# Attention by halves of the queries, with half of the output product fed into it

## The chip, the cores and the metric

The kernel runs on one NeuronCore of a Trainium2 chip. The metric is the device time of one execution in microseconds (us), lower is better. All data are float32.

## The reference, cut to what matters

One hybrid layer on 1024 tokens of width 1024. A norm and one input projection feed two branches: a bidirectional state-space (SSM) branch in chunks of 128, and windowed attention with 16 query heads over 4 key heads. Both are gated and normed, concatenated (2048 columns), multiplied by `w_out` (2048 x 1024), added to the input and normed once more.

```python
h = rms_norm(x, norm_in_g)
z, xbc, dt_raw, q, k, v, ga = split(h @ w_in)
...
def block(idx):                      # 128 queries see 384 keys
    logits = einsum('bqkgd,btkd->bkgqt', qb, kb) * scale + bias
    logits = where(valid, logits, NEG_INF)
    m = maximum(max(logits), sink)
    p = exp(logits - m)
    denom = sum(p) + exp(sink - m)
    return einsum('bkgqt,btkd->bqkgd', p, vb) / denom
...
y_attn = rms_norm(o * silu(ga), attn_norm_g)
return rms_norm(x + concat([y_ssd, y_attn]) @ w_out, final_norm_g)
```

Keys and values of a key head serve 4 query heads. The 8 query blocks of 128 tokens need the keys of their own block and of its two neighbours.

## The kernel before, in words

Engines: TensorE (PE) for matmuls and transposes, VectorE (DVE), ScalarE (ACT), GpSimd (POOL), and SyncE (SP), whose queue issues nearly all DMAs. Each engine and each queue works in order. The orders on DVE, ACT, POOL and SP are set by a planner that simulates the whole program and gives each engine, whenever it is free, the earliest traced instruction that is ready in the simulation. In the attention stage the order on PE is written out by hand: `pe` (L773) ties every matmul behind the one before.

Products are made in float32r: each operand is split into a rounded `hi` and a rest `lo`, and three matmuls (hi hi, hi lo, lo hi) make one product.

Stages:

1. Norm of x, projections by blocks of 128 output columns (`proj_steps`, L147; 24 matmuls of 128x512 per half of the tokens), SSM branch with convolutions. Projections of the gates and of q and k are pulled forward into the SSM stage by `fill`. What comes from the branches goes to DRAM (`z_d`, `ga_d`, `q_d`, `k_d`, `v_d`, `y_d`).
2. Attention: 32 steps, for each key head `kv` (outer) and each query block `qb` (inner). A `Step` loads its queries (`qt`, L824), and per key head `load_kv` (L753) loads keys twice (once for each half of the partitions), values and bias into two rotating buffers; `vz` (L889) holds one half of the values with zeros beside. `logits` (L838): 2 matmuls (L850), DVE adds bias and takes the maximum into `nm` (L853), ACT makes the exponential and its sum into `sm` (L856); four times per step. `denominators` (L859): sink exponential, sum and reciprocal (L861 to L865), once per step. `transpose` (L867), `weigh` (values, L898) and `collect` (L903) into `og`.
3. After every 4 query blocks, `gate(kv, hf)` (L912): the reciprocals are transposed on PE (L917), copied by ACT (L919), written to DRAM from POOL (L920), read back to all partitions (L924), and POOL multiplies gate, reciprocal and `og` (L928, L929), squares (L930) and sums the squares over heads into `sqa` (L933 to L936). `store` (L939) puts `og` to `o_d`; with the last key head it marks the half as stored (`stored`).
4. Output. `outputs` (L640) is a generator. Its first half, 2 x 8 row blocks x 2 halves of the columns with 12 matmuls each, multiplies the SSM part of `w_out` and adds it to `accs`, which hold x. The second half, for each row block `sb`, waits until its half of attention is stored (L694), sums `sqa` over channels (L699), multiplies 48 matmuls (L658) with `o_d` rows that `parts` (L646) splits, adds (L707), squares (L709) and norms (L119 on POOL, L730 on DVE).
5. `chore` (L419) splits 128x512 pieces of `w_out` (ACT L429, DVE L430, loads L416 through three buffers) into the space that the projection's inputs leave: 32 pieces, of which the last 8 may be made only when the SSM half of the product is done (`chores_up_to(32)`, L692).

Each step follows the string `STEP` (L398): `q` logits of the next step, `t` transposes, `w` values, `s` one chore, `g` the gate of a finished half, `d` the denominators of the next step, `c` collect, and `f4` a share of the step's feed. `feed` (L782) pulls matmuls out of the projections that are left and then out of `outputs`, and counts matmuls; `QUOTA` (L393) of them go into each step, and `FIRST` behind each of the four first logits. Whatever is not fed by then follows attention (`feed(100000)`, L985).

```python
    steps = [(kv, qb) for kv in range(NKV) for qb in range(NSB)]
    ...
        if pending and qb % 4 == 2:
            store()
        if qb % 4 == 3:
            done = kv, qb // 4
    ...
    gate(*done)
    store()
    feed(100000)
```

Of the kernel before, what the change touches and what calls it, by code (L numbers as in the profile page):

```python
# [16 lines left out]
P = 128  # L17
# [18 lines left out]
def kernel(  # L36
# [356 lines left out]
    PRE, QUOTA, FIRST, RB = 1, 17, 2, 3  # L393
# [4 lines left out]
    STEP = "q0 q1 f4 t1 s f3 t2 f4 q2 f3 t0 f4 q3 w1 g f4 w2 s f4 d w0 c"  # L398
# [241 lines left out]
    def outputs():  # L640
# [47 lines left out]
        fg = at.tile([P, D], F32, tag="khh", name="fg")  # L688
        nc.sync.dma_start(out=fg, in_=bass.AP(tensor=fin_g.tensor, offset=fin_g.offset, ap=[[0, P], [1, D]]))
        junk = at.tile([P, D], F32, tag="kll", name="junk")  # L690
# [62 lines left out]
    def load_kv(kv):  # L753
        khh = at.tile([P, S], F32R, tag="khh", name="khh")
        kll = at.tile([P, S], F32R, tag="kll", name="kll")
        for t, hl in ((khh, 0), (kll, 1)):
            for half in range(2):
                nc.sync.dma_start(out=t[half * 64:(half + 1) * 64, :].bitcast(F32), in_=k_d[hl, kv])
        vt = at.tile([P, NSB, P], F32R, tag="vt", name="vt")
        nc.sync.dma_start(out=vt.bitcast(F32), in_=v_d[kv].rearrange("b t c -> t b c"))  # L760
        bias = at.tile([P, 2, 320], F32, tag="bias", name="bias")
        for h in range(4):
            r = rep_d[kv * 4 + h, 0:1, 127:447]
            nc.sync.dma_start(out=bias[(h % 2) * 64:(h % 2 + 1) * 64, h // 2, :],
                              in_=bass.AP(tensor=r.tensor, offset=r.offset, ap=[[511, 64], [1, 320]]))
        return khh, kll, vt, bias
# [33 lines left out]
    vz = [at.tile([P, NSB, P], F32R, name=f"vz{i}", bufs=1) for i in range(2)]  # L800
# [10 lines left out]
    def half_tiles(kv, hf):  # L811
        sm = sqp.tile([P, 16], F32, tag="sm", name="sm", bufs=2)
        og = sqp.tile([P, 4, 2, P], F32, tag="og", name="og", bufs=2)
        return sm, og

    class Step:


        def __init__(self, kv, qb):
            self.kv, self.qb = kv, qb  # L820
            if kv not in kvs:
                kvs[kv] = load_kv(kv)
            self.qt = at.tile([P, 2, 4, 64], F32R, tag="qt", name="qt", bufs=2)
            nc.sync.dma_start(out=self.qt.rearrange("p s h q -> p (s h q)").bitcast(F32),  # L824
                              in_=q_d[kv, :, :, 2 * qb:2 * qb + 2].rearrange("i d s h q -> (i d) (s h q)"))
            self.lg = lgs[(kv * NSB + qb) % 2]
            self.nm = at.tile([P, 4], F32, tag="nm", name="nm", bufs=3)
            if qb % 4 == 0:
                halves[kv, qb // 4] = half_tiles(kv, qb // 4)
            self.sm = halves[kv, qb // 4][0].rearrange("p (b c s) -> p b c s", b=2, c=4)[:, :, qb % 4, :]  # L830

            self.lo, self.hi = lo, hi = qb > 0, qb < NSB - 1
            self.groups = [[(256, 384 if lo else 320)],
                           [(0, 128, 0, qb - 1)] * lo + [(128, 256, 0, qb)],
                           [(384, 512, 1, qb)] + [(512, 640, 1, qb + 1)] * hi]
            self.tr = {}

        def logits(self, k):  # L838
            kv, qb = self.kv, self.qb
            khh, kll, vt, bias = kvs[kv]  # L840
# [6 lines left out]
            k0 = (qb - 1) * P + c0  # L847
            ps = bank("s")
            for i, kt in enumerate((khh, kll)):
# [5 lines left out]
                                   accum_out=self.nm[:, k:k + 1])  # L855
            A.activation(out=l, in_=l, func=AF.Exp, scale=-1.0,  # L856
                         bias=self.nm[:, k:k + 1], accum_out=self.sm[:, hp, sub:sub + 1])

        def denominators(self):  # L859
            n2 = self.nm.rearrange("p (b s) -> p b s", b=2)  # L860
            V.tensor_tensor(out=n2, in0=n2, op=ALU.add,  # L861
                            in1=snk[:, 2 * self.kv:2 * self.kv + 2].unsqueeze(2).broadcast_to([P, 2, 2]))
            A.activation(out=self.nm, in_=self.nm, func=AF.Exp)
            V.tensor_tensor(out=self.sm, in0=self.sm, in1=n2, op=ALU.add)
            V.reciprocal(out=self.sm, in_=self.sm)  # L865
# [16 lines left out]
        def weigh(self, i):  # L882
            vt, qb = kvs[self.kv][2], self.qb
            if i == 1:
                self.po = bank("y")
                if qb == 0:
                    for half, t in enumerate(vz):
                        h = slice(half * 64, (half + 1) * 64)
                        nc.sync.dma_start(out=t[h].bitcast(F32), in_=v_d[self.kv, :, h].rearrange("b t c -> t b c"))  # L889

            if i > 0:
                prods = [(g[2], vt[:, g[3], :], j * 256) for j, g in enumerate(self.groups[i])]
            else:
                prods = [(0, vz[0][0:P if self.lo else 64, qb + 1, :], 0)] if self.hi else []
                prods += [(1, vz[1][:, qb - 1, :], 0)] if self.lo else []
# [7 lines left out]
        def collect(self):  # L903
            pov = self.po.rearrange("p (s b a q) -> p b s a q", s=2, b=2, a=2)
            c = self.qb % 4
            og = halves[self.kv, self.qb // 4][1][:, c].rearrange("p b (s q) -> p b s q", s=2)
# [5 lines left out]
    def gate(kv, hf):  # L912
        sm, og = halves[kv, hf]
# [32 lines left out]
    steps = [(kv, qb) for kv in range(NKV) for qb in range(NSB)]  # L946
# [4 lines left out]
    cur.denominators()  # L951
    done = None
    total = sum(int(t[1:]) for t in STEP.split() if t[0] == "f")
    for n, (kv, qb) in enumerate(steps):
        nxt = Step(*steps[n + 1]) if n + 1 < len(steps) else None
        fed = part = 0
        for t in STEP.split():
# [7 lines left out]
            elif t[0] == "d" and nxt:  # L965
                nxt.denominators()
# [72 lines left out]
```

## Time and profile before

| what | us |
|---|---|
| median of 3 runs | 922.18 |
| lowest and highest | 919.39, 931.5 |
| the profiled execution's own time | 922.42 |
| its span in the profile | 920.6 |

The profile is of one execution. Times in it count from the start of the span. An engine's busy time is the sum of its instructions; matmuls are pipelined, so their durations overlap, and the distance from one start to the next is what each takes. "PEld" is PE's loading of weights. "L147" is a line of the kernel, and "<-" after an idle time names what ended it. The granted clock of PE is given as a share of its full speed, over the whole span 0.978.

### The profile page before, as it was taken

Reading aid. Unit: us, or ns where it says so; the run is one execution under the profiler, and the core shown is the slowest. Engines: PE = TensorE matmul, PEld = TensorE weight load, DVE = VectorE, ACT = ScalarE, POOL = GpSimd, SP = SyncE. Lnnn points to the kernel's source line nnn. Section 1 sums busy time; section 2 is a strip of 40 time slices with the busy share of each in tenths; the row PEclk is TensorE's granted clock in tenths of the full one; section 3 lists DMA queues with packets and bytes.
Section 4 is the critical chain, followed back from the end, with each engine's and each line's share of the span. In section 5 each row is a group of like instructions: output and inputs, shape, how many; then the busy total and the mean of one; then the engine's idle time right before and its main releaser. Section 6 shows DMA issues by size and latency. Waiting matters only on the chain.

```text
span 920.6 us, 13289 instructions
## 1 busy us (share of the span) xinstructions
PE 852.7 (93%) x4622; PEld 717.1 (78%) x4622; DVE 652.0 (71%) x1108; ACT 472.8 (51%) x1102; POOL 325.4 (35%) x258
## 2 busy tenths in 40 slices
PE   6799999998699999999979978988889999999997
PEld 5798788886577888888757856867778878888886
DVE  6475674696798466458989815796888998896433
ACT  7442573453566345434745515766656767662222
POOL 2201012645777100245598630140341342345001
PEclk9999999999999999999998998999999999999999
DMA  7232554675768412678868668369838464343321
GB/s 282 63 92 57 190 179 162 210 228 173 224 224 267 114 46 91 186 227 227 258 206 253 190 202 218 98 179 290 245 95 216 122 193 124 111 142 121 106 95 57
DMA packets 137407, 155.67 MB, mean 169 GB/s; under 512 B 44235, under 2 KB 93259, under 8 KB 137212
## 3 DMA queue, kind: packets, MB, share of 16 engines
q1 hardware_dynamic: 135660, 150.30, 53.7%
q0 software_dynamic: 1536, 4.26, 1.8%
q8 instruction: 36, 0.59, 0.3%
q14 instruction: 31, 0.25, 0.1%
q10 hardware_dynamic: 144, 0.26, 0.1%
HBM read 112.49 MB, written 44.40 MB: 170 GB/s over the span
## 4 chain that ended last, share of the span: by engine, by line
PE 67%; DVE 15%; DMA 9%; issue 4%; ACT 2%; SPq 1%; POOL 1%; DVEq 0%; POOLq 0%; ACTq 0%
PE mm L147 34%; PE mm L658 16%; PE y L898 4%; PE s L850 3%; PE mm L284 3%; DMA cb<-cs_d 2%; DMA snk<-in_sink_dram 2%; DMA oraw<-in_w_out_dram 2%; DVE M L583 2%; PE t L873 2%; PE s L533 1%; DVE pl L879 1%; PE s L515 1%; DVE lg L853 1%; DVE M L584 1%
## 5 line engine op out<-in xcount | busy, mean ns | idle before, releaser
L147 PE MATMUL mm<-hlo,whi 128*128 128x512 f32 (+1 forms) x640 | 248.7, 390 | 5.8 <-DVE hlo L210 5.1
L147 PE MATMUL mm<-hhi,whi 128*128 128x512 f32 (+1 forms) x640 | 249.2, 392 | 0.0
L147 PE MATMUL mm<-hhi,wlo 128*128 128x512 f32 (+1 forms) x640 | 248.1, 389 | 0.0
L147 PEld LDWEIGHTS mm<-hlo,whi 128*128 128x128 f32 x640 | 122.7, 192 | 28.7 <-DVE hlo L210 5.8
L147 PEld LDWEIGHTS mm<-hhi,wlo 128*128 128x128 f32 x640 | 122.9, 192 | 21.9 <-issue 0.7
L147 PEld LDWEIGHTS mm<-hhi,whi 128*128 128x128 f32 x640 | 122.5, 192 | 21.6 <-issue 0.7
L658 PE MATMUL mm<-hhi,yh 128*128 128x512 f32 (+1 forms) x264 | 104.0, 394 | 0.0
L658 PE MATMUL mm<-hhi,yl 128*128 128x512 f32 (+1 forms) x264 | 104.0, 394 | 0.0
L658 PE MATMUL mm<-hlo,yh 128*128 128x512 f32 (+1 forms) x264 | 103.9, 394 | 0.0
L856 ACT ACTIVATE lg<-lg,nm 128x320 f32<-128x320 f32 (+2 forms) x128 | 68.9, 539 | 49.5 <-DVE nm L853 47.3
L243 DVE SCALAR_TENSOR_TENSOR acc<-pad,prm_sb,acc 128x1024 f32<-128x1024 f32 x48 | 62.3, 1301 | 27.1 <-ACT acc L240 25.8
L853 DVE CUSTOM_DVE_ANT_0 lg<-s,bias,nsnk 128x320 f32<-128x320 f32 (+2 forms) x128 | 64.5, 517 | 20.5 <-PE s L850 20.3
L138 POOL TENSOR_TENSOR wlo<-wraw,whi 128x1024 fp32r<-128x1024 f32 x12 | 30.7, 2560 | 106.1 <-ACT whi L135 106.1
L135 ACT ACTIVATE whi<-wraw 128x1024 fp32r<-128x1024 f32 x38 | 40.2, 1057 | 49.0 <-PE mm L147 46.7
L574 ACT ACTIVATE cb<-cb,ncs 128x128 f32<-128x128 f32 x128 | 39.3, 389 | 32.8 <-DMA cb<-cs_d 32.7
L138 DVE TENSOR_TENSOR wlo<-wraw,whi 128x1024 fp32r<-128x1024 f32 x26 | 36.9, 1418 | 26.7 <-ACT whi L135 26.5
L658 PEld LDWEIGHTS mm<-hhi,yh 128*128 128x128 f32 x264 | 49.9, 189 | 5.9
L658 PEld LDWEIGHTS mm<-hlo,yh 128*128 128x128 f32 x264 | 49.9, 189 | 5.8
L850 PE MATMUL s<-khh,qt 128*128 128x320 f32 (+1 forms) x128 | 39.5, 314 | 16.0 <-DMA qt<-q_d 10.8
L658 PEld LDWEIGHTS mm<-hhi,yl 128*128 128x128 f32 x264 | 49.9, 189 | 5.6
L879 DVE TENSOR_TENSOR pl<-t,ph 128x512 fp32r<-128x512 f32 (+1 forms) x64 | 41.1, 653 | 5.6 <-ACT ph L878 5.1
L235 POOL MEMSET pad<- 128x2 f32 x12 | 1.4, 117 | 123.1 <-DMA dx_d<-pad 65.3
(223 smaller groups left out, 1825.3 us busy)
## 6 DMA issues: line engine op xcount, KB each, us to landing
wraw<-in_w_blk_dram SPq DMA_DIRECT2D x38, 512.0 KB, 4.1
cb<-cs_d SPq DMA_DIRECT2D x32, 512.0 KB, 5.5
oraw<-in_w_out_dram SPq DMA_DIRECT2D x32, 256.0 KB, 4.5
qt<-q_d SPq DMA_DIRECT2D x32, 256.0 KB, 3.4
et<-es_d SPq DMA_DIRECT2D x56, 128.0 KB, 4.0
dx_d<-pad SPq DMA_DIRECT2D x8, 512.0 KB, 4.3
z_d<-gz SPq DMA_DIRECT2D x16, 256.0 KB, 2.6
yb<-dx_d SPq DMA_DIRECT2D x16, 256.0 KB, 3.1
```

The costliest lines, as they stand in the source:

```text
L135: A.activation(out=hi, in_=raw, func=AF.Copy)
L138: eng.tensor_tensor(out=lo, in0=raw, in1=hi.bitcast(F32), op=ALU.subtract)
L147: yield T.matmul(ps, lhsT=l[:, kb, :], rhs=r[sh][:, kb, cols], start=(n == 0), stop=(n == 3 * NKB - 1))
L243: V.scalar_tensor_tensor(out=acc, in0=pad[:, k:k + S], scalar=cw[:, blk * 6 + k:blk * 6 + k + 1], in1=acc, op0=ALU.mult, op1=ALU.add)
L284: T.matmul(ps[:, 0:288], lhsT=l[sh][:, kb, j * P:(j + 1) * P], rhs=r[:, kb, :], start=(n == 0), stop=(n == 3 * NKB - 1))
L574: A.activation(out=E[:, h, :], in_=E[:, h, :], func=AF.Identity, bias=ncs[:, 0, c, hh:hh + 1])
L658: yield T.matmul(ps[:, cols], lhsT=l[:, j * P:(j + 1) * P], rhs=r[:, dh * 512 + cols.start:dh * 512 + cols.stop], start=first and n == 0, ...
L850: pe(lambda: T.matmul(ps[:, 0:c1 - c0], lhsT=self.qt[:, sub, 2 * hp:2 * hp + 2, :], rhs=kt[:, k0:k0 + c1 - c0], start=(i == 0), stop=(i == ...
L853: V.tensor_tensor_reduce(out=l, in0=ps[:, d0 - c0:d1 - c0], in1=bias[:, hp, d0 - f0:d1 - f0], scale=-1.0, scalar=nsnk[:, sk], op0=ALU.add, ...
L856: A.activation(out=l, in_=l, func=AF.Exp, scale=-1.0, bias=self.nm[:, k:k + 1], accum_out=self.sm[:, hp, sub:sub + 1])
L879: V.tensor_tensor(out=pl[0:w, 0:n], in0=ps[0:w, 0:n], in1=ph[0:w, 0:n].bitcast(F32), op=ALU.subtract)
L898: pe(lambda: T.matmul(self.po[:, sub * 256:(sub + 1) * 256], lhsT=v, rhs=r[0:v.shape[0], c:c + 256], start=i == 1 and n == 0 and j == 0, s ...
```

## The change

The 32 steps run in another order: for the first half of the queries all four key heads, then the same for the second half. Keys, values and bias are loaded per key head and half (5 of 8 blocks of 128 tokens), keys with one DMA for both copies. `nm` becomes one tile of 16 columns per key head and half; `denominators` and its token `d` go, and their four operations stand at the head of `gate`, once for 4 query blocks. `QUOTA` is 22 in place of 17. The final norm's `fg` and `junk` no longer share the key buffers.

```diff
@@ -390,12 +390,12 @@
-    PRE, QUOTA, FIRST, RB = 1, 17, 2, 3
+    PRE, QUOTA, FIRST, RB = 1, 22, 2, 3
     FORWARD = ((1, 1), (1, 1), (0, 1), (1, 1), (1, 1), (0, 1), (1, 1), (1, 1))
-    STEP = "q0 q1 f4 t1 s f3 t2 f4 q2 f3 t0 f4 q3 w1 g f4 w2 s f4 d w0 c"
+    STEP = "q0 q1 f4 t1 s f3 t2 f4 q2 f3 t0 f4 q3 w1 g f4 w2 s f4 w0 c"
     blocks = [(Z0 + b, gate_half(z_d[b])) for b in range(8)]
     blocks += [(K0 + b, qk_half(store_k(b), 1.0)) for b in range(2)]
     for b in range(0, 8, 2):
@@ -685,9 +685,9 @@
         rs_a = const.tile([P, NSB], F32, name="rs_a")
-        fg = at.tile([P, D], F32, tag="khh", name="fg")
+        fg = at.tile([P, D], F32, name="fg", bufs=1)
         nc.sync.dma_start(out=fg, in_=bass.AP(tensor=fin_g.tensor, offset=fin_g.offset, ap=[[0, P], [1, D]]))
-        junk = at.tile([P, D], F32, tag="kll", name="junk")
+        junk = at.tile([P, H2], F32, name="junk", bufs=1)
         allowed[0] = 32
         chores_up_to(32)
         for sb in range(NSB):
@@ -750,14 +750,19 @@
     sqa = sqp.tile([P, NSB, P], F32, name="sqa")
     at = pool(ctx, "at", bufs=2, side="right")
-    def load_kv(kv):
-        khh = at.tile([P, S], F32R, tag="khh", name="khh")
-        kll = at.tile([P, S], F32R, tag="kll", name="kll")
+    KB = 5
+    def load_kv(kv, hf):
+        b0 = 3 * hf
+        khh = at.tile([P, KB * P], F32R, tag="khh", name="khh")
+        kll = at.tile([P, KB * P], F32R, tag="kll", name="kll")
         for t, hl in ((khh, 0), (kll, 1)):
-            for half in range(2):
-                nc.sync.dma_start(out=t[half * 64:(half + 1) * 64, :].bitcast(F32), in_=k_d[hl, kv])
-        vt = at.tile([P, NSB, P], F32R, tag="vt", name="vt")
-        nc.sync.dma_start(out=vt.bitcast(F32), in_=v_d[kv].rearrange("b t c -> t b c"))
+            r = k_d[hl, kv, 0:1, b0 * P:(b0 + KB) * P]
+            nc.sync.dma_start(out=t.bitcast(F32), in_=bass.AP(tensor=r.tensor, offset=r.offset,
+                                                              ap=[[0, 2], [S, 64], [1, KB * P]]))
+        vt = at.tile([P, KB, P], F32R, tag="vt", name="vt")
+        nc.sync.dma_start(out=vt.bitcast(F32), in_=v_d[kv, b0:b0 + KB].rearrange("b t c -> t b c"))
         bias = at.tile([P, 2, 320], F32, tag="bias", name="bias")
         for h in range(4):
             r = rep_d[kv * 4 + h, 0:1, 127:447]
@@ -797,7 +802,7 @@
     done_proj = []
-    vz = [at.tile([P, NSB, P], F32R, name=f"vz{i}", bufs=1) for i in range(2)]
+    vz = [at.tile([P, KB, P], F32R, name=f"vz{i}", bufs=1) for i in range(2)]
     for half, t in enumerate(vz):
         G.memset(t[(1 - half) * 64:(2 - half) * 64].bitcast(F32), 0.0)
@@ -809,25 +814,26 @@
     halves = {}
     def half_tiles(kv, hf):
+        nm = sqp.tile([P, 16], F32, tag="nm", name="nm", bufs=2)
         sm = sqp.tile([P, 16], F32, tag="sm", name="sm", bufs=2)
         og = sqp.tile([P, 4, 2, P], F32, tag="og", name="og", bufs=2)
-        return sm, og
+        return nm, sm, og
     class Step:
         def __init__(self, kv, qb):
             self.kv, self.qb = kv, qb
-            if kv not in kvs:
-                kvs[kv] = load_kv(kv)
+            self.hf, self.b0 = qb // 4, qb // 4 * 3
+            if (kv, self.hf) not in kvs:
+                kvs[kv, self.hf] = load_kv(kv, self.hf)
             self.qt = at.tile([P, 2, 4, 64], F32R, tag="qt", name="qt", bufs=2)
             nc.sync.dma_start(out=self.qt.rearrange("p s h q -> p (s h q)").bitcast(F32),
                               in_=q_d[kv, :, :, 2 * qb:2 * qb + 2].rearrange("i d s h q -> (i d) (s h q)"))
-            self.lg = lgs[(kv * NSB + qb) % 2]
-            self.nm = at.tile([P, 4], F32, tag="nm", name="nm", bufs=3)
+            self.lg = lgs[qb % 2]
             if qb % 4 == 0:
                 halves[kv, qb // 4] = half_tiles(kv, qb // 4)
-            self.sm = halves[kv, qb // 4][0].rearrange("p (b c s) -> p b c s", b=2, c=4)[:, :, qb % 4, :]
+            self.nm, self.sm = halves[kv, qb // 4][:2]
             self.lo, self.hi = lo, hi = qb > 0, qb < NSB - 1
             self.groups = [[(256, 384 if lo else 320)],
@@ -837,14 +843,17 @@
         def logits(self, k):
             kv, qb = self.kv, self.qb
-            khh, kll, vt, bias = kvs[kv]
+            khh, kll, vt, bias = kvs[kv, self.hf]
             hp, sub = divmod(k, 2)
             sk = slice(2 * kv + hp, 2 * kv + hp + 1)
             f0, f1 = 64 * sub, 64 * sub + 320
             c0, c1 = (128, 384) if qb == 0 else (0, 256) if qb == NSB - 1 else (f0, f1)
             d0, d1 = max(f0, c0), min(f1, c1)
-            k0 = (qb - 1) * P + c0
+            k0 = (qb - 1 - self.b0) * P + c0
+            n = 8 * hp + 2 * (qb % 4) + sub
+            nm, sm = self.nm[:, n:n + 1], self.sm[:, n:n + 1]
             ps = bank("s")
             for i, kt in enumerate((khh, kll)):
                 pe(lambda: T.matmul(ps[:, 0:c1 - c0], lhsT=self.qt[:, sub, 2 * hp:2 * hp + 2, :],
@@ -852,17 +861,8 @@
             l = self.lg[:, hp, 320 * sub + d0 - f0:320 * sub + d1 - f0]
             V.tensor_tensor_reduce(out=l, in0=ps[:, d0 - c0:d1 - c0], in1=bias[:, hp, d0 - f0:d1 - f0],
                                    scale=-1.0, scalar=nsnk[:, sk], op0=ALU.add, op1=ALU.min,
-                                   accum_out=self.nm[:, k:k + 1])
-            A.activation(out=l, in_=l, func=AF.Exp, scale=-1.0,
-                         bias=self.nm[:, k:k + 1], accum_out=self.sm[:, hp, sub:sub + 1])
-        def denominators(self):
-            n2 = self.nm.rearrange("p (b s) -> p b s", b=2)
-            V.tensor_tensor(out=n2, in0=n2, op=ALU.add,
-                            in1=snk[:, 2 * self.kv:2 * self.kv + 2].unsqueeze(2).broadcast_to([P, 2, 2]))
-            A.activation(out=self.nm, in_=self.nm, func=AF.Exp)
-            V.tensor_tensor(out=self.sm, in0=self.sm, in1=n2, op=ALU.add)
-            V.reciprocal(out=self.sm, in_=self.sm)
+                                   accum_out=nm)
+            A.activation(out=l, in_=l, func=AF.Exp, scale=-1.0, bias=nm, accum_out=sm)
         def transpose(self, i):
             group = self.groups[i]
@@ -880,19 +880,20 @@
             self.tr[i] = ph, pl
         def weigh(self, i):
-            vt, qb = kvs[self.kv][2], self.qb
+            vt, qb, b0 = kvs[self.kv, self.hf][2], self.qb, self.b0
             if i == 1:
                 self.po = bank("y")
-                if qb == 0:
+                if qb % 4 == 0:
                     for half, t in enumerate(vz):
                         h = slice(half * 64, (half + 1) * 64)
-                        nc.sync.dma_start(out=t[h].bitcast(F32), in_=v_d[self.kv, :, h].rearrange("b t c -> t b c"))
+                        nc.sync.dma_start(out=t[h].bitcast(F32),
+                                          in_=v_d[self.kv, b0:b0 + KB, h].rearrange("b t c -> t b c"))
             if i > 0:
-                prods = [(g[2], vt[:, g[3], :], j * 256) for j, g in enumerate(self.groups[i])]
+                prods = [(g[2], vt[:, g[3] - b0, :], j * 256) for j, g in enumerate(self.groups[i])]
             else:
-                prods = [(0, vz[0][0:P if self.lo else 64, qb + 1, :], 0)] if self.hi else []
-                prods += [(1, vz[1][:, qb - 1, :], 0)] if self.lo else []
+                prods = [(0, vz[0][0:P if self.lo else 64, qb + 1 - b0, :], 0)] if self.hi else []
+                prods += [(1, vz[1][:, qb - 1 - b0, :], 0)] if self.lo else []
             for n, (sub, v, c) in enumerate(prods):
                 for j, r in enumerate(self.tr[i]):
                     pe(lambda: T.matmul(self.po[:, sub * 256:(sub + 1) * 256], lhsT=v,
@@ -903,14 +904,20 @@
         def collect(self):
             pov = self.po.rearrange("p (s b a q) -> p b s a q", s=2, b=2, a=2)
             c = self.qb % 4
-            og = halves[self.kv, self.qb // 4][1][:, c].rearrange("p b (s q) -> p b s q", s=2)
+            og = halves[self.kv, self.hf][2][:, c].rearrange("p b (s q) -> p b s q", s=2)
             A.activation(out=og[0:64], in_=pov[64:128, :, :, 0, :], func=AF.Copy)
             A.activation(out=og[64:128], in_=pov[0:64, :, :, 1, :], func=AF.Copy)
             V.tensor_tensor(out=og[0:64], in0=pov[0:64, :, :, 0, :], in1=og[0:64], op=ALU.add)
             V.tensor_tensor(out=og[64:128], in0=pov[64:128, :, :, 1, :], in1=og[64:128], op=ALU.add)
     def gate(kv, hf):
-        sm, og = halves[kv, hf]
+        nm, sm, og = halves[kv, hf]
+        n2 = nm.rearrange("p (b c) -> p b c", b=2)
+        V.tensor_tensor(out=n2, in0=n2, in1=snk[:, 2 * kv:2 * kv + 2].unsqueeze(2).broadcast_to([P, 2, 8]), op=ALU.add)
+        A.activation(out=nm, in_=nm, func=AF.Exp)
+        V.tensor_tensor(out=sm, in0=sm, in1=nm, op=ALU.add)
+        V.reciprocal(out=sm, in_=sm)
         gt = sqp.tile([P, 2, H2], F32, tag="gt", name="gt", bufs=1)
         nc.sync.dma_start(out=gt, in_=ga_d[2 * kv:2 * kv + 2, :, hf * H2:(hf + 1) * H2].rearrange("b p s -> p b s"))
         ps = bank("t")
@@ -943,12 +950,11 @@
         if kv == NKV - 1:
             stored.add(hf)
-    steps = [(kv, qb) for kv in range(NKV) for qb in range(NSB)]
+    steps = [(kv, 4 * hf + c) for hf in range(2) for kv in range(NKV) for c in range(4)]
     cur = Step(*steps[0])
     for k in range(4):
         cur.logits(k)
         feed(FIRST)
-    cur.denominators()
     done = None
     total = sum(int(t[1:]) for t in STEP.split() if t[0] == "f")
     for n, (kv, qb) in enumerate(steps):
@@ -962,8 +968,6 @@
                 fed = QUOTA * part // total
             elif t[0] == "q" and nxt:
                 nxt.logits(arg)
-            elif t[0] == "d" and nxt:
-                nxt.denominators()
             elif t[0] == "t":
                 cur.transpose(arg)
             elif t[0] == "w":
```

## Rows read from the trace of the kernel before

**Rows 1.** The page, busy time of each engine: us, share of the span, instructions.
```profile
PE 852.7 (93%) x4622; PEld 717.1 (78%) x4622; DVE 652.0 (71%) x1108; ACT 472.8 (51%) x1102; POOL 325.4 (35%) x258
```

**Rows 2.** Busy time by stretch: PE, PEld, DVE, ACT, POOL; granted clock; DMA share.
```profile
556.00:564.00 8.00, 7.55 (x35) 6.54 (x36) 3.53 (x16) 4.17 (x15) 0.00 (x0) 0.77 1.05 253
...
556.00:825.00 269.00, 252.05 (x1476) 214.90 (x1476) 225.37 (x592) 178.94 (x506) 78.91 (x55) 0.98 0.60 168
825.00:870.00 45.00, 45.00 (x207) 37.46 (x207) 25.15 (x37) 13.94 (x30) 14.21 (x12) 1.00 0.38 123
```

**Rows 3.** The chain of waits, its end: start, us, what.
```profile
825.68 43.69 PE mm L658 x192
...
870.15 43.96 PE mm L658 x216
914.14 0.50 DVE acc L707
```

**Rows 4.** Timeline of PE: logits that open steps, the last gate's transpose.
```profile
560.77 0.31 PE L850 MATMUL s<-khh,qt 128*128 128x320 f32 x1
...
666.28 0.30 PE L850 MATMUL s<-khh,qt 128*128 128x320 f32 x1
...
674.02 0.31 PE L850 MATMUL s<-khh,qt 128*128 128x320 f32 x1
...
824.62 0.27 PE L917 MATMUL t<-ident,sm 128*16 128x128 f32 x1
```

**Rows 5.** The chain of waits from 540 to the end, by line.
```profile
by line: PE mm L658 38.7%; PE y L898 9.7%; PE mm L147 9.0%; PE s L850 6.8%; DMA oraw<-in_w_out_dram 4.3%; PE t L873 4.0%; issue 3.3%; DVE pl L879 3.2%; DVE lg L853 2.7%; DVE hlo L430 2.3%; DVE sm L864 1.7%; DVE nm L861 1.4%; ACT lg L856 1.4
```

**Rows 6.** Timeline of ACT, POOL and SP behind the last gate.
```profile
826.82 0.27 ACT L919 ACTIVATE rdt<-t 16x128 f32<-16x128 f32 x1
...
827.37 0.57 POOL L920 DMA_DIRECT2D rd_d<-rdt  x1 [9.26 <-ACT rdt L919]
...
837.85 2.72 POOL L929 TENSOR_TENSOR og<-og,gt 128x1024 f32<-128x1024 f32 x1
...
840.59 0.37 SPq L941 DMA_DIRECT2D o_d<-og  x1
...
844.40 1.63 POOL L936 TENSOR_TENSOR sqa<-sqa,gt 128x512 f32<-128x512 f32 x1
```

**Rows 7.** DMA issues: count, KB each, median us from issue to landing.
```profile
o_d<-og SPq DMA_DIRECT2D x8, 512.0 KB, 3.4
...
y<-o_d SPq DMA_DIRECT2D x16, 256.0 KB, 2.6
...
vz<-v_d SPq DMA_DIRECT2D x8, 256.0 KB, 5.7
```

**Rows 8.** Timeline of SP and PE where attention begins.
```profile
543.46 1.26 SPq L758 DMA_DIRECT2D kll<-k_d  x2
...
556.45 0.55 PE L850 MATMUL s<-khh,qt 128*128 128x256 f32 x1 [10.82 <-DMA qt<-q_d]
...
557.01 0.63 PE L147 MATMUL mm<-hhi,whi 128*128 128x512 f32 x1
557.44 0.63 PE L147 MATMUL mm<-hlo,whi 128*128 128x512 f32 x1
```

**Rows 9.** Groups by line, 556 to 825: busy us, mean ns, idle before, releaser.
```profile
L430 DVE SCALAR_TENSOR_TENSOR hlo<-oraw,prm_sb,hhi 128x512 fp32r<-128x512 f32 x28 | 26.6, 953 | 6.1 <-ACT hhi L429 5.3 <-PE t L917 0.7
...
L861 DVE TENSOR_TENSOR nm<-nm,snk 128x4 f32<-128x4 f32 x32 | 15.6, 489 | 12.2 <-ACT lg L856 12.1
...
L864 DVE TENSOR_TENSOR sm<-sm,nm 128x4 f32<-128x4 f32 x32 | 11.6, 362 | 4.3 <-ACT nm L863 4.1
```

**Rows 10.** Timeline of POOL and DVE, at a gate and the first final norm.
```profile
681.76 2.71 POOL L929 TENSOR_TENSOR og<-og,gt 128x1024 f32<-128x1024 f32 x1
...
682.16 2.34 DVE L861 TENSOR_TENSOR nm<-nm,snk 128x4 f32<-128x4 f32 x1
...
843.10 3.48 DVE L730 SCALAR_TENSOR_TENSOR acc<-acc,frs,fg 128x512 f32<-128x512 f32 x2 [2.33 <-POOL frs L119]
```

## The prediction

> **What bounds the kernel now.** First the page's share of each engine: TensorE (PE) has work in flight 93% of the span, VectorE (DVE) 71%, the others half or less [rows 1]. Such a share is an average over stages, so the next view is the busy time by stretch [rows 2]. Attention and what is fed into it lie from 556 to 825: PE is busy 252.05 of 269 us and DVE 225.37, so 84% of the second engine. From 825 on PE is full: that is the half of the output product that needs attention's results. Third, the chain of work that ended last [rows 3]: behind attention it is nothing but matmuls, 192 in 43.69 us and 216 in 43.96 us (the first 0.23 us each; of the second, 48 are half as wide), and 6.5 us of ending after 914.14. The end has no wait in it at all.
>
> Inside attention I measure one step by the start of its logits in the timeline of PE [rows 4]: 666.28 to 674.02, so 7.75 us when nothing stalls. 24 of the 32 steps are of this kind; the 8 at the sequence's two ends have 2 transposes and 4 value matmuls fewer, some 0.7 us less. That makes 32 x 7.75 - 8 x 0.7 = 242.4 us. The steps really last from 560.77 to the start of the last gate's transpose at 824.62 [rows 4], 263.9 us. So 21.5 us of them are stalls, and that is nearly all that any reordering of attention can win there. Which ones: in the chain from 540 to the end, by line, the denominators' two DVE additions hold 1.7% and 1.4%, the w_out loads 4.3% and the DVE half of their split 2.3% of 381 us [rows 5]. The denominators alone are 3.1% x 381 = 11.8 us of chain.
>
> **The change part by part.**
>
> *Matmuls that move.* Fed before: 8 + 32 x 17 = 552, exactly what there is (168 of the projections, 384 of the SSM half). After: 8 + 32 x 22 = 712, and the second output half may start once half 0 is stored, which is traced at the end of step 18; the 552nd matmul falls in step 24.7, six steps later. So 160 instructions (4 small sums, 156 of 384 products) leave the end and enter the steps. Each costs the 0.23 us of rows 3 wherever PE is the limit: +36.8 us in attention, and a clean step becomes 7.75 + 5 x 0.23 = 8.9 us. PE's work stays the same in all; only waits can change.
>
> *The end.* Before, from the end of the last gate's transpose (824.62 + 0.27 = 824.9) to the end of the span: 95.7 us, in which 196 instructions for rows 0 to 511 lay over the last gate's chain. After, 36 matmuls are left for that: 36 x 0.23 = 8.3 us. That chain in rows 6: the reciprocals leave through POOL at 827.37, are read back and multiplied in; the product that finishes the output rows starts at 837.85 and takes 2.72; the last sum of squares ends at 844.40 + 1.63 = 846.0. The store is issued at 840.59, and a store and a load take 3.4 and 2.6 us to land [rows 7]: 840.6 + 0.4 + 3.4 + 2.6 = 847.0, then the rounding of one tile, some 0.6, and PE may go on at 847.6, 22.7 us behind 824.9. I take 1.7 us off, since ScalarE came to the reciprocals' copy only at 826.82, two w_out splits being ahead of it [rows 6]. So 21 us, 8.3 of them covered, 12.7 with PE idle. Bounds: 17 (the hand-overs between the rows gone) and 25 (other POOL work in between). After an idle time PE runs at half its clock at first: behind 10.82 us without work the matmuls started 0.43 us apart (557.01 to 557.44) [rows 8], and the stretch from 556 to 564 has a granted clock of 0.77 [rows 2], so for nearly half of it the lower level. That cost (1 - 0.77) x 8 = 1.8 us there, and I charge 1.6. The end after: 21 + 43.96 + 6.5 + 1.6 = 73.1 us against 95.7: -22.6 us. Without the wait it would be -36.8; the wait keeps 14 us of what the move gives back.
>
> *Stalls in the steps.* Denominators: 32 sets of three DVE operations and one of ScalarE become 8 sets on four times the columns. Their additions held DVE 15.6 + 11.6 = 27.2 us, with 12.2 + 4.3 us of DVE idle before them [rows 9]; a quarter stays. They are long because they stand behind POOL: the addition at 682.16 took 2.34 us on four columns (the mean is 0.49) while a POOL product ran from 681.76 for 2.71 [rows 10]. Of the chain's 11.8 us, 9 go. What is late next is their neighbours in DVE's queue that also read two SBUF tiles beside POOL; I give 2 us back. The gate's transpose now needs the reciprocals, in PE's fixed order: worked out only when the gate comes, they would cost PE two additions (0.49 + 0.36 by the means), an exponential and a reciprocal, some 1.2 us, 8 times. But the inputs are complete over a step earlier, and before, the addition ran as soon as the last exponential was done (its idle time ends with ACT lg [rows 9]), so I take nothing; the bound is 9.6 us. Longer steps: DVE had 225.4 / 32 = 7.0 us of work per step of 8.2. Of it 0.85 goes with the additions, 0.2 comes back with the eight sets, and the moved products bring what they had at the end, 25.15 us of DVE in a stretch of 45 us with 192 matmuls [rows 2]: 160/192 x 25.15 / 32 = 0.65. So 7.0 of 8.9 us, 79% in place of 84%, and I take 5 us off the stalls of the steps with w_out splits (two per step, 0.95 us each on DVE [rows 9]). Against that, the last 8 splits are made in one go where the second output half begins. Before, that was at the end, beside 24 matmuls; after, it is step 24.7, in the midst of attention: 8 x 0.95 = 7.6 us of DVE through three buffers. Price between 0 and 10 us; I take 4, since two steps' slack on DVE is 2 x 1.9 us. Sum: -9 + 2 - 5 + 4 = -8 us, 13.5 us of stalls left. Bounds: -16 and +5.
>
> *Loads.* Per key head and half 7 issues in place of 9 per key head (one for both copies of the keys), and vz twice as often: 8 x 9 = 72 issues against 4 x 11 = 44, 28 x 0.6 = 17 us more in SP's queue, spread over 280 us and hidden by two buffers that come free some four steps ahead; without that cover a head change would wait for a landing like vz's, 5.7 us [rows 7]. Before the first logits the query load waits in SP's queue behind the first key loads, and two issues fewer at 0.63 [rows 8] make -1.2 us; bounds -5 and +3, since the order there is the planner's. The vz load may start only when the step before has used it and must land before the next step's last matmuls: 1.2 + 5.7 = 6.9 us against 8.9, so hidden, eight times instead of four; if SP stands elsewhere, up to 2 us at each of 7 turns. Of the three PSUM banks for products the output rows now hold two for 2.2 steps while a transpose group needs one per step: taken as nothing, up to 3 us. The final norm's gain and scratch get buffers of their own: an earlier load, no cost.
>
> **Sum.** +36.8 - 22.6 - 8 - 1.2 = +5.0 us on the profiled execution's own 922.42 (its span is 920.6, so 1.8 lie around it): 927.4 us. The median of the runs shown is 922.18, 0.2 below the profiled one. 2% of the time, 18 us, is about what a measurement of this kernel can tell from no change.
>
> **The rivals.**
> (a) *The stalls nearly vanish.* With 8.9 us of PE per step DVE is never late; then -16 instead of -8, and the last gate without contention takes 18 us, so the end wins 25.6: 36.8 - 25.6 - 16 - 1.2 = -6, 916 us. For it: the clean steps of rows 4. Against it: POOL still holds DVE at every gate, and the w_out loads are as late as before.
> (b) *POOL's queue stops DVE: slower.* The final norm of rows 0 to 383 now runs inside attention. Its power is a POOL operation, and the DVE product behind it waits in order. At the end before, DVE idled 2.33 us there, behind a gate's products on POOL, with PE far ahead [rows 10]. Inside attention, all that the next step needs of DVE is queued behind that product. A gate holds POOL from its first product to its last sum for some 11 us (837.85 is the second of five, 846.0 the end [rows 6]); gates come at steps 24 and 28, norms at about 27, 29 and 31. Two collisions at 9 us make +18: 945 us. It decides, as slower by 2%, from two of them on; one makes 936.
> (c) *PE has room, and the moved matmuls are free.* Weight loads fill only 214.90 of 269 us in attention [rows 2], 80%; were the rest room, 54 us would take the 36.8 us for nothing: -22.6 - 1.2 = -24, 898 us. Against it: from 825 to 870, where one matmul follows the other without a gap, the loads fill 37.46 of 45 us, 83% [rows 2]; so 80% is nearly full. The Trainium skill (Perfetto Trace Analysis, Identifying the Most-Contended Engine) has TensorE's headroom judged by weight loading and not by matmul time, and read as free time that would be this rival. The trace does not agree here: 83% was as far as it went with no gap at all.
> (d) *The second output half does not start in attention*, since its rows come too late: the end and its cover stay, and -8 - 1.2 = -9 leaves 913 us. By the code the store is six steps early.
>
> **How the numbers follow.** My forecast 0.52, (a) 0.24, (b) 0.16, (c) 0.04, (d) 0.04. The forecast's own range, by the end's wait (17 to 25) and some 5 us of stalls either side, is 918 to 937. The whole range reaches into (a) and (d) below, and above to between one collision and two: 911 to 943 us. Faster by over 2% (under 904) is (c) and a little of (a) with an earlier start: 0.05. Slower (over 941) is most of (b) and the upper end of the forecast: 0.14. Within 2%: 0.81.
>
> **What would show it.** Right: clean steps of about 8.9 us; attention some 28 us longer (269 to about 297); PE idle for 9 to 16 us behind the last gate, ended by the sum of squares or by the loaded output rows, then some matmuls 0.43 us apart; 6.5 us from the last product to the end, as now; the denominators' additions under 9 us of DVE. Wrong: no gap at the end (then the gate's chain is under 10 us, or the order differs), steps of 8.2 us on average (c), DVE idle for over 5 us before a norm's product (b), or PE waiting for vz or for the reciprocals at each gate.

## The result and the profile after

| | before | changed |
|---|---|---|
| median, us | 926.61 | 1002.29 |
| lowest to highest | 919.39 to 931.5 | 999.74 to 1003.3 |
| span of the profiled execution | 920.6 | 1000.7 |

The changed kernel is slower: ratio 1.0819, 95% interval 1.0729 to 1.091. The forecast was 927.4 with a range of 911 to 943. Something costs 75 us that no term of the prediction and none of its rivals holds.

The views in the order in which they lead there. First the busy time by stretch (columns as in [rows 2]): the steps, the wait behind the last gate, the rest.

```profile
565.00:927.00 362.00, 303.22 (x1636) 257.23 (x1636) 223.08 (x549) 186.47 (x504) 81.95 (x59) 0.90 0.49 145
927.00:948.00 21.00, 9.77 (x45) 7.98 (x43) 9.97 (x11) 3.10 (x8) 12.03 (x10) 0.78 0.35 109
948.00:995.00 47.00, 46.45 (x219) 39.15 (x219) 16.68 (x32) 10.00 (x23) 3.95 (x5) 0.95 0.21 69
```

The second and third stretch are much as forecast: 21 us behind the last gate, in which PE is busy 9.77 and so idles 11.2 (forecast 12.7), then 216 matmuls. The first is not: 362 us in place of 269 [rows 2], with PE busy 84%, DVE 62% and ScalarE 52%. No engine is the bound of the steps, and the DMA engines are no fuller than before, 0.49 against 0.60. All of them wait. For what, the waits of PE from 540 on say (us in total, times, the longest):

```profile
PE s L859 <- DMA qt<-q_d: 25.7, 2, 18.9
PE y L899 <- DMA vz<-v_d: 20.0, 5, 6.9
PE y L899 <- ACT ph L878: 16.7, 3, 8.0
PE t L699 <- POOL sqa L943: 11.2, 1, 11.2
PE t L873 <- ACT lg L865: 9.9, 2, 7.4
```

Only the fourth and, of the first, some 10 us for the first queries were in the prediction. The third and the last end on ScalarE, but ScalarE was itself waiting, for the `w_out` loads: `ACT hhi L429 <- DMA oraw` has 49.0 us in 10 waits, where it had 15.1 in 8 before. So loads of three kinds (queries, vz, `w_out`) come late, and their shapes did not change except for vz, which got smaller. What they share is SP's queue. The chain of waits from 540 to the end (start, us, what) names what stands in it:

```profile
543.75 16.73 DMA vt<-v_d
...
603.61 15.34 DMA kll<-k_d
...
704.40 17.52 DMA kll<-k_d
...
747.24 16.32 DMA kll<-k_d
...
793.17 18.29 DMA kll<-k_d
```

The first piece is a load of values right behind two key loads; the others are key loads, and one takes 15 to 18 us from issue to landing. Now it has 320 KB in one DMA; before, it had 256 KB (count, KB each, median us to landing):

```profile
khh<-k_d SPq DMA_DIRECT2D x8, 256.0 KB, 5.2
kll<-k_d SPq DMA_DIRECT2D x8, 256.0 KB, 7.2
```

And SP's own timeline where attention begins, beside PE's first logits (start, us):

```profile
543.19 0.52 SPq L762 DMA_DIRECT2D kll<-k_d  x1
543.75 5.34 SPq L765 DMA_DIRECT2D vt<-v_d  x1
549.14 5.38 SPq L769 DMA_DIRECT2D bias<-rep_d  x3
...
561.18 1.06 SPq L831 DMA_DIRECT2D qt<-q_d  x2
...
564.86 0.55 PE L859 MATMUL s<-khh,qt 128*128 128x256 f32 x1 [18.94 <-DMA qt<-q_d]
```

Before, the issue of values stood there as

```profile
544.77 0.59 SPq L760 DMA_DIRECT2D vt<-v_d  x1
```

Behind the two merged key loads it holds SP for 5.34 us in place of 0.59. The query load is issued at 561.18, and PE, which had waited 10.82 us before [rows 8], waits 18.94.

### The profile page after: what moved, and what is told of

Same layout as the page of the kernel before. It is cut to its first block, busy times and chain, and to the rows that moved or that the text cites. A ratio compares the mean times of both kernels' runs of the same rounds, so it can differ in the third digit from the quotient of the medians.

```text
span 1000.7 us, 13339 instructions
## 1 busy us (share of the span) xinstructions
PE 870.4 (87%) x4622; PEld 731.3 (73%) x4622; DVE 634.0 (63%) x1036; ACT 469.3 (47%) x1078; POOL 325.0 (32%) x258
## 4 chain that ended last, share of the span: by engine, by line
PE 47%; DMA 26%; DVE 11%; POOL 4%; SPq 4%; issue 4%; ACT 3%; POOLq 0%; DVEq 0%; ACTq 0%
PE mm L147 24%; PE mm L658 11%; DMA kll<-k_d 7%; DMA oraw<-in_w_out_dram 3%; DMA vz<-v_d 3%; PE mm L284 3%; DMA cb<-cs_d 2%; PE y L899 2%; PE s L859 2%; DMA et<-es_d 2%; DMA snk<-in_sink_dram 2%; DMA vt<-v_d 2%; PE t L873 2%; DVE M L583 1%; DVE M L584 1%
## 5 line engine op out<-in xcount | busy, mean ns | idle before, releaser
L147 PEld LDWEIGHTS mm<-hlo,whi 128*128 128x128 f32 x640 | 123.2, 193 | 28.8 <-DVE hlo L210 5.6
L658 PE MATMUL mm<-hhi,yh 128*128 128x512 f32 (+1 forms) x264 | 107.9, 409 | 0.0
L658 PE MATMUL mm<-hlo,yh 128*128 128x512 f32 (+1 forms) x264 | 107.3, 407 | 0.0
L658 PE MATMUL mm<-hhi,yl 128*128 128x512 f32 (+1 forms) x264 | 107.1, 406 | 0.0
L859 PE MATMUL s<-khh,qt 128*128 128x320 f32 (+1 forms) x128 | 41.6, 329 | 25.7 <-DMA qt<-q_d 25.7
L927 POOL DMA_DIRECT2D rd_d<-rdt x8 | 4.8, 598 | 164.2 <-ACT rdt L926 164.2
L658 PEld LDWEIGHTS mm<-hhi,yh 128*128 128x128 f32 x264 | 52.0, 197 | 5.8
L430 DVE SCALAR_TENSOR_TENSOR hlo<-oraw,prm_sb,hhi 128x512 fp32r<-128x512 f32 x32 | 26.4, 837 | 45.0 <-ACT hhi L429 44.7
```

Source lines behind the costliest of these rows:

```text
L147: yield T.matmul(ps, lhsT=l[:, kb, :], rhs=r[sh][:, kb, cols], start=(n == 0), stop=(n == 3 * NKB - 1))
L430: V.scalar_tensor_tensor(out=lo[:, c:c + 512], in0=raw, scalar=gain, in1=hi[:, c:c + 512].bitcast(F32), op0=ALU.mult, op1=ALU.subtract)
L658: yield T.matmul(ps[:, cols], lhsT=l[:, j * P:(j + 1) * P], rhs=r[:, dh * 512 + cols.start:dh * 512 + cols.stop], start=first and n == 0, ...
L859: pe(lambda: T.matmul(ps[:, 0:c1 - c0], lhsT=self.qt[:, sub, 2 * hp:2 * hp + 2, :], rhs=kt[:, k0:k0 + c1 - c0], start=(i == 0), stop=(i == ...
```

## The experiments

The kernel before ran beside each of them on the same chip; its medians there were 924.1 to 926.3, and ratios are to those runs.

**1. Keys by two DMAs again.**

```diff
-            r = k_d[hl, kv, 0:1, b0 * P:(b0 + KB) * P]
-            nc.sync.dma_start(out=t.bitcast(F32), in_=bass.AP(tensor=r.tensor, offset=r.offset,
-                                                              ap=[[0, 2], [S, 64], [1, KB * P]]))
+            for half in range(2):
+                nc.sync.dma_start(out=t[half * 64:(half + 1) * 64, :].bitcast(F32),
+                                  in_=k_d[hl, kv, :, b0 * P:(b0 + KB) * P])
```

> The changed kernel with the keys loaded as before, by one DMA for each half of the partitions (64 rows of 640), nothing else undone. Theory K (the one DMA with a leading dimension of 2 is slow and holds up SP's queue and all loads behind it): the waits of PE on loads go, and the time is what was predicted but for its own errors, 915 to 940 us, with 10 to 13 us of idle PE at the last gate left. Rival R1 (order and halves: twice as many loads of values, bias and zero-padded values crowd the queue, whatever the shape of the key DMA): 985 to 1005 us. Rival R2 (the splits of w_out and the fed matmuls make DVE and ACT the bound): 985 to 1005 us too, with idle PE ended by ACT and DVE.

Measured: 927.34 us, ratio 1.0036 (1.0012 to 1.006). All of the 75 us hang on these lines. Of the 76.7 us between the two spans (1000.7 and 924.0), 8.1 lie before the first logits, 67.9 between them and the last gate, and 0.7 behind it. Its DMA issues (count, KB each, median us to landing):

```profile
khh<-k_d SPq DMA_DIRECT2D x16, 160.0 KB, 4.2
kll<-k_d SPq DMA_DIRECT2D x16, 160.0 KB, 5.3
```

and its waits of PE from 540 on:

```profile
PE t L699 <- POOL sqa L943: 10.7, 1, 10.7
PE s L859 <- DMA qt<-q_d: 9.1, 1, 9.1
PE y L899 <- DVE pl L879: 5.4, 7, 2.0
PE y L899 <- ACT ph L878: 3.1, 1, 3.1
```

No wait of PE for vz is left, and ScalarE's waits for the `w_out` loads fall from 49.0 to 14.1 us, although these loads are issued as often as in the changed kernel. R1 and R2 fall.

**2. The slow load put into the kernel before.**

```diff
-                nc.sync.dma_start(out=t[half * 64:(half + 1) * 64, :].bitcast(F32), in_=k_d[hl, kv])
+            nc.sync.dma_start(out=t.bitcast(F32), in_=bass.AP(tensor=r.tensor, offset=r.offset,
+                                                              ap=[[0, 2], [S, 64], [1, S]]))
```

> The kernel before, with its keys loaded by one DMA for both copies (leading dimension 2, stride 0, 64 rows of 1024). Theory K: each of the 8 loads takes some 25 to 30 us to land (1024 in place of 640 columns; 16 us at 640), the first logits start some 20 us later, and the time is 940 to 970 us, although the later key heads are loaded eight steps ahead. Rivals R1 and R2: as before, 917 to 932 us.

Measured: 983.0 us, ratio 1.0623 (1.0587 to 1.0659). The same load slows the kernel before as well, and by more than the 940 to 970 us that I had expected of 8 loads, most of them issued far ahead. PE waits 48.2 us in 5 waits for query loads, the longest 26.8 at the first logits: they stand in the queue behind the key loads or between two of them, and it does not help that the later keys are not needed for steps yet.

**3. One DMA, 128 rows that follow each other.**

```diff
+            r = k_d[hl, kv // 2 * 2, 0:1, b0 * P:(b0 + KB) * P]
...
+                                                              ap=[[S, 128], [1, KB * P]]))
```

> The changed kernel with one DMA per key tile as changed, but from 128 rows that follow each other (the second half of the partitions gets the keys of the neighbouring head, so these logits are of other keys; bytes, destination and number of DMAs are as changed). Theory K in the form that the leading dimension of 2 is to blame, and not the merging or the size: landing in 4 to 7 us, time 915 to 940 us. If one larger DMA is slow as such: 15 us and more to land, time 985 to 1005 us.

Measured: 927.43 us, ratio 1.0012 (0.9985 to 1.0039); DMA issues:

```profile
khh<-k_d SPq DMA_DIRECT2D x8, 320.0 KB, 4.5
kll<-k_d SPq DMA_DIRECT2D x8, 320.0 KB, 5.6
```

One DMA of 320 KB lands nearly as fast as one of 160 KB, and one or two DMAs make the same time. Merging is harmless; the shape `[[0, 2], [S, 64], ...]` is not.

**4. A leading dimension of 2 that steps, and one of 4.** Both keep one DMA of 128 rows and change only which rows.

```diff
+ap=[[128 * S, 2], [S, 64], [1, KB * P]]
...
+ap=[[64 * S, 4], [S, 32], [1, KB * P]]
```

> The changed kernel with its one DMA per key tile, whose leading dimension of 2 now steps over two key heads instead of by 0 (the second half of the partitions gets the keys of another head, so these logits are of other keys; no byte is read twice in one DMA). If the count of the leading dimension is what makes the load slow: 985 to 1010 us, as changed. If reading the same bytes twice is (a stride of 0): 915 to 940 us.

> The same with a leading dimension of 4 (32 rows of each of the four key heads; again other keys, same bytes and destination). If the data of one DMA go over only as many DMA engines as the leading dimension counts, a load takes half the time of the changed one, 8 to 9 in place of 16 to 18 us, and the time lies between, 930 to 965 us. If any shape that does not merge into one run of rows is slow: 985 to 1010 us.

Measured: 1002.99 us with the step over two heads, as the changed kernel, so that reading the same bytes twice is not the cause. 962.48 us with a leading dimension of 4, ratio 1.0417 (1.0336 to 1.0498), about half of the loss. Its chain of waits shows two key loads, at 8 and 13 us:

```profile
563.65 8.09 DMA khh<-k_d
...
685.26 13.45 DMA kll<-k_d
```

So it is the count of the leading dimension: 2 gives 15 to 18 us, 4 gives 8 to 13, 64 and 128 give 4 to 6. The packets in the traces say how. Every one of these key loads has 128 packets of 2560 bytes, one for each row, and a packet takes a median of 0.10 to 0.11 us whether the dimension counts 2, 4 or 128. What differs is how many of them are under way at once, on average over the time in which any is: 2.0 with a leading dimension of 2, with stride 0 as with the step over two heads, 3.7 with 4, and 7.9 with 128 rows. So the two loads of a pair (`khh` and `kll`) take some 14 to 15 us one behind the other in the changed kernel, and 3 to 6 us with 128 rows. That fits as many DMA engines as the leading dimension counts; on which engine a packet ran, no trace says. The share of the 16 DMA engines in a stretch in which keys are loaded (column before the last), for 2, for 4 and for 128 rows:

```profile
606.00:617.00 11.00, 11.00 (x68) 9.48 (x67) 7.19 (x22) 7.07 (x21) 2.07 (x1) 1.00 0.34 101
804.00:813.00 9.00, 9.00 (x54) 7.75 (x53) 7.95 (x21) 6.50 (x17) 0.00 (x0) 1.00 0.70 160
769.00:773.00 4.00, 4.00 (x26) 3.51 (x25) 3.23 (x9) 2.71 (x8) 0.00 (x0) 1.00 1.01 362
```

Other loads move in these stretches too. With 2, the engines are busy for a third of the stretch, although other loads wait behind the keys.

**5. The slow loads on another queue.**

```diff
-            nc.sync.dma_start(out=t.bitcast(F32), in_=bass.AP(tensor=r.tensor, offset=r.offset,
+            nc.gpsimd.dma_start(out=t.bitcast(F32), in_=bass.AP(tensor=r.tensor, offset=r.offset,
```

> The changed kernel with its slow key loads (leading dimension 2) issued from POOL's queue instead of SP's, shape and bytes as changed. If most of the 75 us is other loads standing behind them in SP's queue: 920 to 950 us. If it is the keys' own landing, or the DMA engines that all queues share: 980 to 1005 us.

Measured: 955.92 us, ratio 1.0329 (1.0282 to 1.0375), a little over the first answer's range. The median landing of the slow load, which the profile of the changed kernel does not give, stands here for POOL's queue (us, last column), with what lies on SP's queue:

```profile
khh<-k_d POOLq DMA_DIRECT2D x8, 320.0 KB, 14.8
kll<-k_d POOLq DMA_DIRECT2D x8, 320.0 KB, 16.1
...
vt<-v_d SPq DMA_DIRECT2D x8, 320.0 KB, 8.3
bias<-rep_d SPq DMA_DIRECT2D x32, 80.0 KB, 10.1
vz<-v_d SPq DMA_DIRECT2D x16, 160.0 KB, 8.0
```

So 46 of the 75 us go when the slow loads leave SP's queue (1002.3 - 955.9), and the other loads no longer stand behind them. The other 29 stay: values, bias and vz still land in 8 to 10 us where the third run has 4.8 to 5.7, so the slow loads delay loads on another queue too. How much of the 29 that makes is not shown, as this run may have a cost of its own: POOL, which works in order, waits 45.5 us in 4 waits until it may issue key loads.

**6. Fewer matmuls per step**, keys by two DMAs throughout: `QUOTA` 22, 21, 20, 19, 17.

> As the first run, and 20 matmuls per step in place of 22: 648 fed in attention, so 100 of the first half's are left for the last gate, 23 us against its 20 us. Theory W (the wait at the last gate is the price of feeding too much): PE has no gap over 2 us there, no matmuls at half clock behind it, and the time is 8 to 14 us under the first run. Rival: the end is bound by something else (loads of rows, DVE), and the time is within 4 us of the first run.

> As the first run with 21 matmuls per step: 680 fed, 68 left for the last gate, 15.6 us against some 20. If end and stalls were the only terms: 4 us of idle PE at the last gate, time between the runs with 22 and 20 matmuls, 919 to 925 us (ratio 0.994 to 1.000).

> With 19 matmuls per step: 616 fed, no wait at the end. By the stalls (14 us at 22 matmuls, 24 us at 20) each matmul less per step adds 3 to 5 us of stalls, and with no wait left to win the time is 2 to 6 us over the run with 20: 922 to 927 us (0.997 to 1.003). Rival (the stalls do not hang on the fill): as with 20, 920 us.

> With 17 matmuls per step as before, so the new order, the halves' loads and the denominators per half are all that differs from before; nothing is moved out of the end. If the order costs nothing by itself: as the run with the old order and denominators per half, ratio 0.994 to 1.000. If loads twice as often cost: 1.005 and more.

| matmuls per step | 22 | 21 | 20 | 19 | 17 |
|---|---|---|---|---|---|
| median, us | 927.34 | 923.43 | 920.44 | 917.36 | 916.05 |
| ratio to before | 1.0036 | 0.9973 | 0.9959 | 0.991 | 0.9898 |
| 95% interval | 1.0012 to 1.006 | 0.9947 to 0.9998 | 0.9934 to 0.9985 | 0.9879 to 0.9941 | 0.9866 to 0.993 |
| stalls in the steps, us | 14.1 | about 22 | 24.1 | 20.8 | 18.0 |

The stalls are the gaps on PE over what each matmul takes, from the first logits to the last gate; before they are 23.1 by the same sum. It is good to some 2 us, as it hangs on what counts as a gap. With 21 PE waits 3.6 us at the last gate, near the 4 expected. With 20 that gap is gone, as theory W says, and the time falls by 7 us, just less than the 8 to 14 it asked, as 10 us of other stalls came up (PE waits 8.6 us for `nm`, of which the first run lists nothing; 5.6 for `pl`, against 5.4). My expectation for 19, that less fill means more stalls, was wrong: the stalls follow no line. Each count also gives another order on DVE and ScalarE, which may be why; that is not shown. What is clear is the direction from 22 to 19 and 17: the less is moved, the better. The version with 17 beats both kernels, the one before by 1%. That is more than expected (a ratio of 0.994 to 1.000), and what the new order gains beside the denominators has no run of its own. It has no wait at its end, here by stretch:

```profile
555.00:817.00 262.00, 252.42 (x1475) 217.39 (x1475) 208.10 (x519) 174.87 (x482) 79.07 (x55) 0.97 0.66 187
817.00:862.00 45.00, 45.00 (x208) 37.39 (x207) 25.63 (x37) 14.04 (x31) 14.22 (x12) 1.00 0.40 123
862.00:907.00 45.00, 44.21 (x219) 37.46 (x218) 18.54 (x37) 10.42 (x26) 4.46 (x6) 1.00 0.23 76
```

Beside [rows 2]: 262 us of attention in place of 269, with DVE at 208.10 in place of 225.37, and the same end. Of the 8.1 us that its span is shorter, 6.5 lie between the first logits and the last gate and 1.4 before.

**7. The denominators by themselves**, put back per step in the new order, and worked out per half in the old one.

```diff
+    def denominators(self):
+            nm, sm = (t.rearrange("p (b c s) -> p b c s", b=2, c=4)[:, :, self.qb % 4, :] for t in (self.nm, self.sm))
...
+                nxt.denominators()
```

> As the first run (keys by two DMAs, 22 matmuls per step), but the denominators per step as before, in the new order. My step of the prediction (9 us of chain go, 2 come back at the neighbours): 5 to 9 us over the first run, 932 to 937 us, and stalls in the steps up from 14 to some 20 us. Rival (the blocks behind POOL only move to the next operation): within 2 us of the first run.

> The kernel before, its order and its 17 matmuls per step, with the denominators worked out once per half in the gate. By the prediction's step: 5 to 9 us under the kernel before, 917 to 921 us, as nothing is given back at the end. Rival: within 2 us of before; or slower, if PE waits for the reciprocals at each gate (up to 9.6 us).

Measured: per step in the new order 933.48 us, ratio 1.0118 (1.0051 to 1.0185) against 1.0036 without, so 6 to 8 us, as expected, though the two intervals touch (the first run's reaches 1.006); 19.8 us of stalls against 14.1. Per half in the old order 920.77 us against 924.09, ratio 0.9962 (0.9926 to 0.9998): 3 to 4 us, which is less than the 5 to 9 expected. Groups by line of the seventh run, then of the first (busy us, mean ns, idle before):

```profile
L872 DVE TENSOR_TENSOR sm<-sm,nm 128x4 f32<-128x4 f32 x32 | 14.3, 447 | 7.2 <-ACT nm L871 7.1
L869 DVE TENSOR_TENSOR nm<-nm,snk 128x4 f32<-128x4 f32 x32 | 11.7, 365 | 9.3 <-ACT lg L865 9.1
```

```profile
L919 DVE TENSOR_TENSOR sm<-sm,nm 128x16 f32<-128x16 f32 x8 | 3.2, 403 | 2.3 <-ACT nm L918 2.3
L917 DVE TENSOR_TENSOR nm<-nm,snk 128x16 f32<-128x16 f32 x8 | 3.2, 396 | 2.8 <-ACT lg L865 2.7
```

26.0 us of additions against 6.4: the mean of one is nearly the same at 16 columns as at 4, and a quarter of the sets costs a quarter. The mean is made by a few long ones: the addition to `nm` has a median of 0.163 us and a longest of 2.34 in the seventh run, which fits an operation held up beside POOL [rows 10].

## Why the prediction was wrong

The step that failed is in *Loads*: "two issues fewer at 0.63 [rows 8] make -1.2 us; bounds -5 and +3". I counted the issues of the merged key load and took a landing like that of vz, 5.7 us, for the worst that a head change would wait for, without asking how the rows of this load are laid out. The load has a leading dimension of 2, and took 15 to 18 us. With nothing else different it is worth 75 us (1002.29 against 927.34); 46 of them go with the loads that stand behind it in its queue, and 29 stay when it is issued from another. The trace of before has no load of this shape, so this was a cost to be bounded from far rows, and a bound of 3 us did not do that. A rule for it was at hand: the Trainium skill (DMA: Bandwidth & Descriptors, Rules for kernel authors) says that a DMA whose outermost dimension counts fewer than 16, "e.g. a leading zero-stride broadcast of c copies", is confined to at most c DMA engines. The runs agree on the count (2.0 and 3.7 packets under way with 2 and 4) and on the indifference to the stride. The landing grew by some three times (14.8 us on POOL's queue against 4.5 with 128 rows in one run), not by the 8 that two engines in place of 16 would give if the engines were all of it: with 128 rows 7.9 packets were under way on average, not 16, and each landing also holds the time from the issue to the first packet, 1 to 4 us in the two traces.

The other steps, read in the first run, which has them without this load:

- *The end*: forecast 73.1 us from the end of the last gate's transpose, against 95.7 before, so -22.6. Measured 924.0 - 851.3 = 72.7, so -23.0, with PE idle 10.7 us in one wait (forecast 12.7), ended by the sum of squares, and matmuls 0.43 us apart behind it. By stretch (columns as in [rows 2]; the granted clock is 0.76 in the wait):

```profile
556.00:851.00 295.00, 285.70 (x1635) 245.29 (x1636) 227.75 (x550) 186.44 (x504) 81.53 (x59) 0.98 0.63 179
851.00:872.00 21.00, 10.33 (x48) 8.56 (x46) 9.14 (x11) 3.10 (x8) 11.88 (x9) 0.76 0.37 117
872.00:924.00 52.00, 45.76 (x217) 38.49 (x216) 17.66 (x35) 11.23 (x26) 4.54 (x6) 0.93 0.21 70
```

- *Matmuls that move and stalls*: forecast +36.8 - 8 = +28.8 for the steps. Measured from the first logits to the last gate 294.2 us (556.8 to 851.04) against 268.2 (556.45 to 824.62): +26.0. Stalls 14.1, from 23.1 by the same sum, so -9.0; forecast -8, to 13.5. Of what that -8 is made of, only the denominators have runs: forecast 7 us, measured 6 to 8 in the new order and 3 to 4 in the old. The price for the last splits made in one go, 4 us with bounds 0 and 10, shows in one run: with 21 matmuls PE waits 6.9 us where they are made.
- *Start*: forecast -1.2, for two key issues fewer. The first run has them back, and its first logits start 0.35 us later than before. The third run, with one DMA for each key tile, has them 3.1 us earlier (553.36), inside the bounds. The order of the queue's first issues alone moves this start: 554.2 to 557.9 us in the runs with two key loads.
- *Sum*: +26.0 - 23.0 + 0.35 = +3.4 us of span, forecast +5.0; in the third run it is +2.8 (923.4 against 920.6).

So the three other terms of the sum were right within 3 us each, though the items inside the stalls were mostly not measured by themselves. Of the rivals, (a) did not come, with 14 us of stalls left. (b) did not come at its price: in the changed kernel DVE waited 5.5 us in 5 waits for the norm's power on POOL, the longest 2.8, and 6.9 in 7 before. (c) falls with the fill: going from 17 to 22 per step adds 32.5 us to the steps (261.7 to 294.2) while their stalls fall by some 2 to 4, so the 160 matmuls cost some 35 to 36 us, close to their full 0.23 each. (d) did not come. What I did not draw from my own sum is that the move itself loses: it puts 32.5 us into the steps to take 22.8 off the end, and without it (17 per step, keys by two DMAs) the change is a gain of 1%.

## What to carry to other kernels

Price a DMA by its shape before its bytes: look at the outermost dimension of its source, and where it counts 2 or 4 take it for two to three times slower, as here, and everything behind it in its queue as late. Two DMAs with 64 rows each, or one with 128 rows in one run, were equally good; a short first dimension, as a broadcast over two copies makes it, is the trap. And moving work out of a tail into a stage where the same engine was already full won nothing here, and lost the cover that the tail's last dependency had.

## What was not expected of the hardware

- A DMA of 320 KB to 128 partitions landed in 4.5 to 5.6 us (medians) with 128 rows in one run, in 15 to 18 us on SP's queue and 14.8 to 16.1 on POOL's with a leading dimension of 2, and in 8 to 13 us with 4. Its packets of 0.10 us were under way 7.9, 2.0 and 3.7 at a time. A stride of 0 or not made no difference (1002.29 and 1002.99 us of kernel time).
- Behind two such loads SP needed 5.34 us for an issue that took 0.59 before: a slow load held up the queue's issues too, not only its data.
- Four-fold fewer, four-fold wider additions cost DVE a quarter (6.4 against 26.0 us), as their mean length hardly changed with their width (0.40 against 0.37 and 0.45).
